# Output stage: loading the second token group's attention outputs earlier, and spacing its f16 forms

## The chip, the cores and the metric

The kernel runs on one core of a Trainium2 chip. The metric is the device time of one execution in microseconds (us). Five engines run side by side, each working through its own list of instructions in order: TensorE (PE in the profile; PEld are its weight loads), VectorE (DVE), ScalarE (ACT), GpSimd (POOL) and SyncE (SP), whose work here is to issue DMA transfers. An instruction that must wait for another engine holds up everything behind it in its own list. The kernel writes these lists itself, so the order of instructions on each engine is fixed when the program is built.

## The reference

One block of a bidirectional encoder: x is 2048 tokens of width 1024. A projection feeds two attention mixers, SiLU gates and merge gates. The change touches only the end:

```python
ya = ya.reshape(bsz, S, A_WIDTH) * jax.nn.silu(ga)      # attention outputs A
...
yb = yb.reshape(bsz, S, B_WIDTH) * jax.nn.silu(gb)      # attention outputs B
br_a = ya @ w_branch_a[layer]
br_b = yb @ w_branch_b[layer]
gates = jax.nn.sigmoid(mg.reshape(bsz, S, N_BRANCHES, D).astype(jnp.float32)
                       + b_merge[layer].astype(jnp.float32)).astype(x.dtype)
merged = gates[:, :, 0] * br_a + gates[:, :, 1] * br_b
x = x + merged @ w_out[layer]
```

## The kernel before

**Stages.** The first two thirds project the input and run the attention. Then the gates are computed from the projections (lines 1600 and 302, ended by the tanh of line 1526, and stored to DRAM as `mgd` from line 1530). The last stage, called the tail here, makes the two branch products, merges them, and makes the output product. The gated attention outputs lie transposed in DRAM as `ytd`, the weights of the branches in SBUF as the first parts of `bigh` and `bigl`, the output weights in DRAM as `wod`.

**Number format.** Every f32 matrix that enters a product is split into a high and a low f16 part, and a product is three f16 products. ScalarE makes the high part by scaling and rounding (`hi`, line 1757), VectorE the low part by subtracting the high part from the scaled value (`lo`, line 1761).

**Seven products for eight.** A block product of 2 x 2 blocks is made with seven products of sums of blocks. The right-hand blocks of a branch are two token halves by two channel halves, so a *token group* `s` (0 to 7) is the 128 tokens from 128 s and the 128 tokens from 1024 + 128 s. For each group and branch (s, k), `load` brings two tiles of 256 KB from `ytd` (line 1742), `sums` makes four sums of blocks on VectorE (line 1753, in two `tq` tiles), and seven pairs `hi`, `lo` make the seven forms. The forms `y0` of branch 0 and `y1` of branch 1 each have a ring of eight tiles. A form of group s + 1 therefore takes the tile of an earlier form, and waits until the product that read it is through. The two loaded tiles of branch k lie behind the weights in `WB[k]` and are overwritten by the next group's load, once all sums and forms of the group before are made.

**The order of products.** `Branch(s, k)` has seven products of 24 matmuls (line 1912), `Out(s)` seven products of 12 matmuls (line 1984). `run` interleaves them: products 5 and 6 of one part come between the first products of the next. The order is Branch(0, 0), Branch(0, 1), Branch(1, 0), Branch(1, 1), then for each s Out(s), Branch(s + 2, 0), Branch(s + 2, 1).

**What follows a product.** Some products end in a PSUM bank that a later one adds to. ScalarE copies a bank (`copy`, line 1834, into a `t` or `r` tile), VectorE adds a later state of a bank to it (`add`, line 1845), GpSimd multiplies with the gate tile `g` (line 1922), VectorE adds up the branches (`merge`, line 1929, and `last`, line 1933). `m_build` then makes the sums (line 1949) and forms (`mf`, lines 1953 and 1957) of the merged values for Out. Out's results are added to the tokens `xr` (`put`, line 1991) and stored (line 1994). A product whose bank is still to be copied or added waits.

**What sets the order.** Up to the gates' end a planner (`Plan`, `pl.add(name, engine, us, needs, rank, f)`) places steps: it starts a step when its needs are met and its engine is free, and picks by rank among those that could start. After that `at(t, f)` puts a step at a time written by hand, relative to `pos[0]`, where TensorE stands in the plan. Both only order the instructions in each engine's list: nothing waits for a time when the kernel runs. `y_steps(0, k)` plans group 0; `y_build(s, k, b, b0)` puts the load at `b0` (or at `b`), the sums from `b + Y_S` (4.0), and the forms 0.7 apart.

SP's list at the end of the gates is, in order: the load of (0, 1), three stores of gates, the four gate tiles of (0, 0) (line 1897, which can only start when the last gate product has read its weights, since they lie in the same memory), the loads of (1, 0) and (1, 1), the gate tiles of (0, 1), a last gate store, and then the seven 1 MB parts of the output weights (`wo_load`, line 1890) between gate tiles and tokens.

Of the kernel before, what the change touches and what calls it, by code (L numbers as in the profile page):

```python
# [30 lines left out]
S = 2048  # L31
# [14 lines left out]
def unit_order():  # L46
    us = [("A", 0, 0)]
    for p in range(4):
# [34 lines left out]
W_RAW, L_LAST = 14.0, 0.3  # L83
STD, W_EARLY, G_TH, G_SI, G_CP, K_AT = 5.2, 24.0, 2.0, 4.0, 1.0, (4, 17)
Y_S = 4.0
M_AT = {0: (1.0, (5.0, 6.6, 8.2, 9.8, 11.4, 13.0, 14.6)), 1: (1.0, (6.5, 8.7, 10.9, 13.1, 15.3, 17.5, 19.7)),
        7: (.7, (3.5, 5.4, 7.3, 9.2, 11.1, 13.5, 26.4))}
X_LD = ("g", 0, 1, 2, 3, "w0", 4, 5, "w1", 6, 7, 8, 9, 10, 11, 12, 13, "u")
# [18 lines left out]
def block_kernel(tc, x, w_units, w_gate, w_mrg, w_out, w_bra, w_brk, gain, qkg, sink, bias_a, bias_b, b_merge, out):  # L107
# [273 lines left out]
    def at(t, f, *args):  # L381
        seq[0] += 1
        heapq.heappush(heap, (t, seq[0], f, args))
# [3 lines left out]
    def until(t):  # L387
        while heap and heap[0][0] <= t:
            now[0], _, f, args = heapq.heappop(heap)
            f(*args)  # L390
# [121 lines left out]
    class Order:  # L512
# [17 lines left out]
        def run(self):  # L530
            while self.steps:
                best = {}
                for n, s in self.steps.items():
                    t = self.start(n)
                    if t is not None:
                        best.setdefault(s[0], []).append((t, s[3], n))
                eng, c = min(best.items(), key=lambda e: min(e[1])[0])
                t0 = min(c)[0]
                t, _, n = min((x for x in c if x[0] <= t0 + (0 if eng == "T" else X_US["look"])), key=lambda x: x[1])
                eng, us, _, _, f, args, _ = self.steps.pop(n)  # L540
                self.end[n] = self.free[eng] = t + us
                at(t, f, *args)
# [3 lines left out]
    n = 0  # L546
# [11 lines left out]
    for t in range(NT):  # L558
# [9 lines left out]
        for h in range(2):  # L568
            k = 2 * t + h
# [108 lines left out]
    class Pair:  # L678
# [85 lines left out]
        def hi(self):  # L764

            n = 2 * self.nh
            self.q = self.rw[:, :n * HD].rearrange("p (s h e) -> p s h e", s=2, e=HD)
            A.activation(self.sp[:, :, :self.nh, 0, :], self.q, AF.Copy)  # L768

        def lo(self):  # L770
            sp, nh = self.sp, self.nh
            V.tensor_tensor(sp[:, :, :nh, 1, :], self.q, sp[:, :, :nh, 0, :], OP.subtract)  # L772
# [456 lines left out]
    while t < NPAIR or heap or any(k >= t for k in fill):  # L1229
# [24 lines left out]
        pos = t  # L1254
# [38 lines left out]
    def tq():  # L1293
        return tp.tile([128, 512], F32, name="tq", bufs=2)
# [32 lines left out]
    class Plan:  # L1327
# [23 lines left out]
        def run(self):  # L1351
# [9 lines left out]
            for _ in range(len(self.steps)):  # L1361
# [20 lines left out]
    g_us = G_US  # L1382
    first = 0.0
    GR = 7 * MM
    pl = Plan({"fps": 8, "t2": 4, "tq": 2, "r2": 3, "t4": 3, "raw": 3, "w": 2, "yr": 4, "pc": 7},
              {"w": [[], [("p", 1, i) for i in range(7)]]})
# [347 lines left out]
    def y_parts(s, k):  # L1734

        r = {}

        def load():
            r[0] = y = [WB[k][h][:, 7168:].bitcast(F32).rearrange("p (c t) -> p c t", c=4) for h in range(2)]
            for h in range(2):  # L1740
                t0 = 128 * s + 1024 * h
                nc.sync.dma_start(out=y[h], in_=ytd[4 * k:4 * k + 4, :, t0:t0 + 128].rearrange("c p t -> p c t"))

        def sums(n):
            if n == 0:
                y = r[0]
                a11, a12, a21, a22 = y[0][:, 0:2], y[0][:, 2:4], y[1][:, 0:2], y[1][:, 2:4]
                u, v = (tq()[:].rearrange("p (s c n) -> p s c n", s=2, c=2) for _ in range(2))
                r[1] = (a11, u[:, 0], a12, u[:, 1], v[:, 1], v[:, 0], a22)
                r[2] = ((u[:, 0], a21, a22, OP.add), (u[:, 1], u[:, 0], a11, OP.subtract),  # L1750
                        (v[:, 1], a12, u[:, 1], OP.subtract), (v[:, 0], a11, a21, OP.subtract))
            o, a, b, op = r[2][n]
            V.tensor_tensor(o, a, b, op)

        def hi(i):
            yf[s, k, i] = f = yp.tile([128, 2, 2, 128], F16, name=f"y{k}")
            A.activation(f[:, 0], r[1][i], AF.Copy, scale=ysg[:])

        def lo(i):
            f = yf[s, k, i]  # L1760
            V.scalar_tensor_tensor(f[:, 1], r[1][i], ysg[:], f[:, 0], OP.mult, OP.subtract)

        return load, sums, hi, lo

    def y_build(s, k, b, b0=None):
        load, sums, hi, lo = y_parts(s, k)
        at(b if b0 is None else b0, load)
        for n in range(4):
            at(b + Y_S + .4 * n, sums, n)
        for n in range(7):  # L1770
            at(b + Y_S + .9 + .7 * n, hi, n)
            at(b + Y_S + 1.7 + .7 * n, lo, n)

    def y_steps(s, k):
        load, sums, hi, lo = y_parts(s, k)
        N = lambda *x: ("y", s, k) + x
        r = first + GR * LAST + 4 * STD + 2 * 7 * MM1 * s + 7 * MM1 * k
        pl.add(N("ld"), "S", 2 * g_us["dma"], [("wb", k, 0)] + [n + ("st",) for n in silus], r - 20, load, lag=4.5)
        for n in range(4):
            rel = [N("l", i) for i in range(7)]  # L1780
            pl.add(N("s", n), "V", g_us["a2"], [N("ld"), "yp"] + ([N("s", n - 1)] if n else []), r - 12 + .1 * n, lambda n=n: sums(n),
                   ring=[("tq", rel)] * 2 if n == 0 else ())
        for n in range(7):
            d = {1: 0, 3: 1, 4: 2, 5: 3}.get(n, 0)
            pl.add(N("h", n), "A", g_us["h2"], [N("s", d), "y2"] + ([N("h", n - 1)] if n else []), r - 9 + n, lambda n=n: hi(n))
            pl.add(N("l", n), "V", g_us["l2"], [N("h", n)], r - 8 + n, lambda n=n: lo(n))
# [8 lines left out]
           [("w", dc, "l", i) for dc in list(groups_of)[1:] for i in range(7)], 0, swap_y)  # L1795
    for k in range(2):
        y_steps(0, k)
    pl.run()
    while not end7:
        until(heap[0][0])  # L1800
    pos = [end7[0] + .01]
    y_build(1, 0, pos[0] + 6.0, pos[0] + .1)
    y_build(1, 1, pos[0] + 14.0, pos[0] + .2)
    until(pos[0])

    class Seven:
# [71 lines left out]
    def flush():  # L1878
        while pending:
            pos[0] += .3  # L1880
            late()
# [17 lines left out]
    class Branch(Seven):  # L1899
        n, mm_us = 7, MM1  # L1900
# [37 lines left out]
    def m_build(s, b):  # L1938
# [19 lines left out]

        d, e = M_AT[s if s in (0, 7) else 1]
        for n in range(4):  # L1960
# [5 lines left out]
    class Out(Seven):  # L1966
        n, mm_us = 7, MM
# [39 lines left out]
    def AB(s):  # L2007
        p = pos[0]
        at(p + (4.0 if s else 1.0), g_tiles, s, 1)
        if s == 0:  # L2010
            at(p + 9, g_tiles, 1, 0)
            for i in range(7):
                at(p + 2.0 + 5.5 * i, wo_load, i)
        run(Branch(s, 0))
        run(Branch(s, 1))

    AB(0)
    at(pos[0] + 9, outs[0].load, ((0, 0), (1, 1), (0, 1), (1, 0)))
    AB(1)
    for s in range(8):  # L2020
        p = pos[0]
        if s < 6:
            at(p + .1, g_tiles, s + 2, 0)
            y_build(s + 2, 0, p + 5.0)
            y_build(s + 2, 1, p + 14.0)
        if s < 7:
            at(p + (24.0 if s < 6 else 2.0), outs[s + 1].load, ((0, 0), (1, 1)))
            at(p + (31.0 if s < 6 else 15.5), outs[s + 1].load, ((0, 1),))
            at(p + (31.1 if s < 6 else 28.0), outs[s + 1].load, ((1, 0),))
        if s == 6:  # L2030
            flush()
        run(outs[s])
        if s < 6:
            AB(s + 2)
# [79 lines left out]
```

## Time and profile before

| | us |
|---|---|
| three runs: median (lowest to highest) | 1920.43 (1917.46 to 1922.58) |
| the profiled execution: its time | 1923.34 |
| the profiled execution: its span in the trace | 1920.9 |

The time of the profiled execution is 2.4 us above its span, which counts from its first to its last instruction. The tail fills the last 309 us of the span. Its first part by stretches of 10 us (busy time of each engine in each, and the share of the core's 16 DMA engines that was in use):

| stretch, us from the start | TensorE | VectorE | ScalarE | GpSimd | DMA share |
|---|---|---|---|---|---|
| 1600 to 1610 (gates) | 10.00 | 2.63 | 4.75 | 0.00 | 0.67 |
| 1610 to 1620 | 10.00 | 3.13 | 4.28 | 1.85 | 0.68 |
| 1620 to 1630 | 10.00 | 7.46 | 5.21 | 3.52 | 0.88 |
| 1630 to 1640 | 8.49 | 9.93 | 4.15 | 4.25 | 1.02 |
| 1640 to 1650 | 8.39 | 9.90 | 6.29 | 3.34 | 1.07 |
| 1650 to 1660 | 10.00 | 9.79 | 0.00 | 3.55 | 1.09 |
| 1660 to 1670 | 10.00 | 7.46 | 5.29 | 1.14 | 0.37 |
| 1670 to 1680 | 7.04 | 9.93 | 5.74 | 1.44 | 0.69 |

In a row of the timeline the columns are the start, the duration, the engine, the line, the operation, what it writes and reads, how many instructions are merged in the row, and in brackets the idle time of the engine before it with what ended it. Names in it are those of the tiles without their numbers.

### The profile page before, as it was taken

The numbers are of one execution on the slowest core, as the hardware profiler recorded it, in microseconds if no ns is written. First come the engines' busy times: TensorE is split into PE (matmuls) and PEld (weight loads), VectorE is DVE, ScalarE is ACT, GpSimd is POOL, SyncE is SP. The second block draws the span as 40 slices with busy tenths as digits, with TensorE's granted clock in tenths as the row PEclk, the third lists the DMA queues.
The fourth block names the chain that finished last, engine by engine and source line by source line (L and its number), as shares of the span: only waits on it lengthen the run. The fifth ranks groups of instructions, "written<-read, shape, count | busy, mean of one in ns | idle before, by whom it ended". The sixth has DMA issues, their size and how long they took to land.

```text
span 1920.9 us, 51094 instructions
## 1 busy us (share of the span) xinstructions
PE 1876.6 (98%) x19242; PEld 1439.4 (75%) x19242; DVE 1501.5 (78%) x3835; ACT 1251.2 (65%) x3015; POOL 579.1 (30%) x1363
## 2 busy tenths in 40 slices
PE   6999999999999999999999999999999999899998
PEld 4568987789999899988999898544444446676774
DVE  7679878986887889878789888657778644977885
ACT  8477768887777777777767766575675865433441
POOL 1034333443553435543455445200000001222121
PEclk9999999999999999999999999999999999999999
DMA  6259998988888679887888777776576557854551
GB/s 255 83 98 197 165 183 143 190 169 165 166 150 182 138 156 202 153 157 175 146 169 160 137 148 146 180 295 181 182 214 181 183 186 252 270 153 120 148 153 61
DMA packets 639351, 326.21 MB, mean 170 GB/s; under 512 B 459264, under 2 KB 589952, under 8 KB 636672
## 3 DMA queue, kind: packets, MB, share of 16 engines
q1 hardware_dynamic: 638960, 322.70, 72.6%
q8 instruction: 150, 2.46, 0.6%
q14 instruction: 97, 0.79, 0.2%
q10 hardware_dynamic: 144, 0.26, 0.0%
HBM read 139.08 MB, written 73.66 MB: 111 GB/s over the span
## 4 chain that ended last, share of the span: by engine, by line
PE 86%; DMA 6%; DVE 4%; ACT 2%; issue 1%; SPq 1%; POOL 0%; DVEq 0%; POOLq 0%
PE pj L695 42%; PE fps L1600 17%; PE fps L1984 7%; PE fps L1912 6%; PE s L845 5%; PE pv L894 4%; DMA pt<-p 2%; PE pj L350 2%; PE pj L302 1%; PE fps L302 1%; DMA kq<-spl 1%; DMA bigl<-ytd 1%; PE pt L958 1%; DMA bigl<-sd 1%; PE s L480 0%
## 5 line engine op out<-in xcount | busy, mean ns | idle before, releaser
L695 PE MATMUL pj<-wl,XH 128*128 128x128 f16 (+2 forms) x2816 | 715.9, 268 | 0.0
L695 PE MATMUL pj<-wh,XL 128*128 128x128 f16 (+2 forms) x2816 | 712.2, 269 | 0.0
L695 PE MATMUL pj<-wh,XH 128*128 128x128 f16 (+2 forms) x2816 | 709.4, 268 | 0.0
L695 PEld LDWEIGHTS <-XH 128*128 128x128 f16 x5632 | 575.4, 112 | 54.6
L695 PEld LDWEIGHTS <-XL 128*128 128x128 f16 x2816 | 316.0, 112 | 24.0
L860 DVE CUSTOM_DVE_ANT_0 pr<-s,b,ubuf 128x256 f32<-128x256 f32 (+3 forms) x512 | 218.9, 465 | 42.1 <-PE s L845 39.5
L877 DVE SCALAR_TENSOR_TENSOR p<-pr,p 128x512 f16<-128x512 f32 (+2 forms) x256 | 195.8, 765 | 51.5 <-ACT p L873 48.6
L762 POOL TENSOR_TENSOR rw<-rw,g 128x128 f32<-128x128 f32 (+1 forms) x224 | 149.2, 686 | 202.5 <-DVE rw L755 170.2
L1922 POOL TENSOR_TENSOR g<-g,t 128x512 f32<-128x512 f32 x32 | 48.5, 1515 | 529.5 <-DVE t L1845 529.5
L1600 PEld LDWEIGHTS <-wh 128*128 128x128 f16 x1064 | 104.2, 99 | 123.5 <-issue 0.6
L713 ACT ACTIVATE rw<-pj 128x256 f32<-128x256 f32 (+1 forms) x224 | 87.4, 390 | 130.0 <-PE pj L695 129.3
L777 POOL COPY spl<-spl 128x256 f16<-128x256 f16 (+1 forms) x224 | 96.7, 461 | 244.5 <-DVE spl L772 244.5
L873 ACT ACTIVATE p<-pr 128x512 f16<-128x512 f32 (+2 forms) x256 | 157.7, 616 | 14.6 <-DMA pt<-p 10.3
L1912 PE MATMUL fps<-y,bigh 128*128 128x128 f16 x1792 | 153.8, 219 | 3.9 <-DVE r L1845 3.9
L1984 PE MATMUL fps<-WO,mf 128*128 128x512 f16 x672 | 151.9, 382 | 3.8 <-DVE xr L1991 3.8
L1912 PE MATMUL fps<-y,bigl 128*128 128x128 f16 x896 | 151.8, 219 | 0.0
L845 PE MATMUL s<-kq 128*128 128x128 f16 (+1 forms) x1856 | 148.2, 218 | 3.6 <-DMA kq<-spl 2.7
L1912 PEld LDWEIGHTS <-bigh 128*128 128x128 f16 x1792 | 139.1, 98 | 11.6 <-issue 4.3
L845 PEld LDWEIGHTS <-kq 128*128 128x128 f16 x2016 | 130.9, 98 | 19.9 <-issue 4.5
L894 PE MATMUL pv<-vt,pt 128*128 128x65 f16 (+1 forms) x2784 | 131.9, 193 | 8.1 <-DMA pt<-p 7.4
L894 PEld LDWEIGHTS <-pt 128*128 128x128 f16 x3024 | 119.3, 98 | 24.1 <-DMA pt<-p 12.1
L768 ACT ACTIVATE spl<-rw 128x512 f16<-128x512 f32 (+1 forms) x112 | 72.0, 643 | 80.3 <-POOL vt L724 70.2
(252 smaller groups left out, 3816.7 us busy)
## 6 DMA issues: line engine op xcount, KB each, us to landing
wraw<-in_w_units_dram SPq DMA_DIRECT2D x56, 384.0 KB, 4.8
g<-mgd SPq DMA_DIRECT2D x64, 256.0 KB, 4.9
wraw<-in_w_mrg_dram SPq DMA_DIRECT2D x45, 256.0 KB, 4.2
mgd<-t SPq DMA_DIRECT2D x43, 256.0 KB, 2.9
zd<-z SPq DMA_DIRECT2D x128, 66.0 KB, 2.0
zz<-zd SPq DMA_DIRECT2D x64, 132.0 KB, 3.4
xt<-in_x_dram SPq DMA_DIRECT2D x16, 512.0 KB, 8.2
ytd<-yo SPq DMA_DIRECT2D x32, 256.0 KB, 3.3
```

What stands on the lines that cost most here:

```text
L695: out.append(lambda lhs=lhs, rhs=rhs, ch=ch, a=a, b=b, k=k: T.matmul(ps[:, a:b], lhsT=lhs[:, ch, :], rhs=rhs[:, ch, a:b], start=(k == 0), ...
L713: A.activation(self.rw[:, n * i:n * i + n], self.ps[i][:, :n], AF.Copy)
L762: G.tensor_tensor(q[:, i, :un.nq, :], q[:, i, :un.nq, :], g, OP.mult)
L777: G.tensor_copy(sp[:, i, nh:, :, :], sp[:, i, nq:nh, ::-1, :])
L845: T.matmul(self.sv[j][:, o:o + k1 - k0], lhsT=q[:, h, :], rhs=kt[:, un.nq + kh + v * un.nk, k0:k1], start=(v == 0), stop=(v == 1))
L860: V.tensor_tensor_reduce(out=self.pv[:, j, self.p0:self.p0 + W], in0=self.sv[j], in1=un.bias[:, self.h0 + j, self.b0:self.b0 + W], scale=I ...
L873: A.activation(self.sp[:, :128 * n], self.pr, AF.Copy, scale=PSC)
L877: V.scalar_tensor_tensor(self.sp[:, 128 * n:], self.pr, PSC, self.sp[:, :128 * n], OP.mult, OP.subtract)
L894: T.matmul(self.po[:, j, :w], lhsT=p[:, n * j + s, :], rhs=un.v[key][:, vh, c0:c0 + w], start=(k == 0 and s == 0), stop=(k == 2 and s == n ...
L1600: T.matmul(b[k][:], lhsT=w[:, i, ch, :], rhs=xform(PROD[i][0], lo, ch, q), start=(i < 3 and n == 0), stop=(n == 11), skip_group_check=True)
L1912: out.append(lambda p=p, c=c, wl=wl, yl=yl, n=n: T.matmul(ps[:, 128 * p:128 * p + 128], lhsT=w[wl][:, i, c, p, :], rhs=y[:, yl, c, :], sta ...
L1984: out.append(lambda p=p, ml=ml, wl=wl, k=k: T.matmul(ps[:], lhsT=m[:, ml, p, :], rhs=WO[:, i, wl, p, :], start=(fresh and k == 0), stop=(k ...
```

## The change

The loads of (1, 0) and (1, 1) become planner steps on SP that need only the seven low forms of (0, k), with a rank that puts them behind all other work that could be issued. The sums and forms of group 1 are no longer placed by `y_build`. For (1, 0) the sums stand from 0.2 after the gates' end and the forms from 0.9, 1.6 apart; for (1, 1) from 13.0 and 14.0, 1.6 apart. In the loop over s, the load of (s + 2, 0) moves from 5.0 to 0.05 after the start of Out(s), which is ahead of the gate tiles at 0.1. The constants of `wo_load` get a name and keep their values.

```diff
+Y_1 = (.2, .9, 1.6), (13.0, 14.0, 1.6)
+WO_AT = 2.0, 5.5
...
     for k in range(2):
         y_steps(0, k)
+    ahead = [y_parts(1, k) for k in range(2)]
+    for k in range(2):
+        pl.add(("y", 1, k, "ld"), "S", 2 * g_us["dma"], [("y", 0, k, "l", i) for i in range(7)], 1e4 + k, ahead[k][0], lag=4.5)
     pl.run()
...
     pos = [end7[0] + .01]
-    y_build(1, 0, pos[0] + 6.0, pos[0] + .1)
-    y_build(1, 1, pos[0] + 14.0, pos[0] + .2)
+    for (load, sums, hi, lo), (a, b, d) in zip(ahead, Y_1):
+        for n in range(4):
+            at(pos[0] + a + .2 * n, sums, n)
+        for n in range(7):
+            at(pos[0] + b + d * n, hi, n)
+            at(pos[0] + b + d * n + .8, lo, n)
...
-                at(p + 2.0 + 5.5 * i, wo_load, i)
+                at(p + WO_AT[0] + WO_AT[1] * i, wo_load, i)
...
-            y_build(s + 2, 0, p + 5.0)
+            y_build(s + 2, 0, p + 5.0, p + .05)
             y_build(s + 2, 1, p + 14.0)
```

SP's list at the gates' end, from the second of the three gate stores on (`ytd` into `bigh`, `bigl` is a load of attention outputs, `mgd` from `t` a gate store, `g` from `mgd` gate tiles), before:

```order
L1530 DMA mgd<-t_27977 128x512
L1530 DMA mgd<-t_28007 128x512
L1897 DMA g<-mgd 128x4x128 x4
L1742 DMA bigh<-ytd 128x4x128
L1742 DMA bigl<-ytd 128x4x128
```

and now, with line numbers that the diff has moved:

```order
L1532 DMA mgd<-t_27977 128x512
L1744 DMA bigh<-ytd 128x4x128
L1744 DMA bigl<-ytd 128x4x128
L1532 DMA mgd<-t_28009 128x512
L1906 DMA g<-mgd 128x4x128 x4
```

The load of (1, 0) has moved past one gate store and four gate tiles; the load of (1, 1) follows the gate tiles as before.

VectorE's list after the last form of (0, 1) (`y0` are forms of branch 0, the lines 1845 and 1854 the `add`), before:

```order
L1845 TENSOR_TENSOR t2_28092<-fps_28122,t2_28092 128x512
L1845 TENSOR_TENSOR t2_28174<-fps_28093,t2_28174 128x512
L1753 TENSOR_TENSOR tq_28277<-bigl_27732 128x256
L1753 TENSOR_TENSOR tq_28277<-tq_28277,bigh_27731 128x256
L1753 TENSOR_TENSOR tq_28278<-bigh_27731,tq_28277 128x256
L1845 TENSOR_TENSOR r2_28121<-fps_28053,r2_28121 128x512
L1753 TENSOR_TENSOR tq_28278<-bigh_27731,bigl_27732 128x256
L1761 SCALAR_TENSOR_TENSOR y0_28300<-bigh_27731,ubuf_70,y0_28300 128x256
L1845 TENSOR_TENSOR t2_28228<-fps_28293,t2_28228 128x512
```

and now:

```order
L1755 TENSOR_TENSOR tq_28061<-bigl_27732 128x256
L1755 TENSOR_TENSOR tq_28061<-tq_28061,bigh_27731 128x256
L1755 TENSOR_TENSOR tq_28062<-bigh_27731,tq_28061 128x256
L1755 TENSOR_TENSOR tq_28062<-bigh_27731,bigl_27732 128x256
L1763 SCALAR_TENSOR_TENSOR y0_28083<-bigh_27731,ubuf_70,y0_28083 128x256
L1763 SCALAR_TENSOR_TENSOR y0_28127<-tq_28061,ubuf_70,y0_28127 128x256
L1854 TENSOR_TENSOR t2_28100<-fps_28133,t2_28100 128x512
```

and, behind four more forms and `add`s, up to the first sum of (1, 1):

```order
L1763 SCALAR_TENSOR_TENSOR y0_28269<-tq_28062,ubuf_70,y0_28269 128x256
L1854 TENSOR_TENSOR r2_28132<-fps_28055,r2_28132 128x512
L1763 SCALAR_TENSOR_TENSOR y0_28310<-bigl_27732,ubuf_70,y0_28310 128x256
L1854 TENSOR_TENSOR t2_28248<-fps_28315,t2_28248 128x512
L1755 TENSOR_TENSOR tq_28362<-bigl_27874 128x256
```

The four sums and seven forms of (1, 0) now stand between the forms of (0, 1) and the fourth `add`; the sums of (1, 1) follow it at once. Before, six low forms of (1, 0) and three other instructions came between that `add` and the sums of (1, 1). ScalarE's list changes in the same way: it now reads (lines 1759 are `hi`, 1843 are `copy`)

```order
L1759 ACTIVATE y0_28083<-bigh_27731,ubuf_70 128x256
L1843 ACTIVATE t2_28100<-fps_28055 128x512
L1759 ACTIVATE y0_28127<-tq_28061,ubuf_70 128x256
L1843 ACTIVATE r2_28132<-fps_28101 128x512
L1759 ACTIVATE y0_28162<-bigh_27731,ubuf_70 128x256
L1843 ACTIVATE t2_28189<-fps_28055 128x512
```

where five copies stood together ahead of the first high form of (1, 0). SP's list at the start of Out(0), before and now:

```order
L1890 DMA WO<-wod 128x4096
L1897 DMA g<-mgd 128x4x128 x4
L1890 DMA WO<-wod 128x4096
L1742 DMA bigh<-ytd 128x4x128
L1742 DMA bigl<-ytd 128x4x128
```

```order
L1899 DMA WO<-wod 128x4096
L1744 DMA bigh<-ytd 128x4x128
L1744 DMA bigl<-ytd 128x4x128
L1906 DMA g<-mgd 128x4x128 x4
L1899 DMA WO<-wod 128x4096
```

The load of (2, 0) has moved past four gate tiles and one part of the output weights. In the later groups it has moved past the four gate tiles in the same way.

## The prediction

> **What bounds the kernel now.** I began with the busy shares of the page.
>
> ```profile
> PE 1876.6 (98%) x19242; PEld 1439.4 (75%) x19242; DVE 1501.5 (78%) x3835; ACT 1251.2 (65%) x3015; POOL 579.1 (30%) x1363
> ```
>
> TensorE works 98% of the span, so a change of order can win only what it loses. For the part that the diff touches, the view of waits from 1611 to 1681 us has two rows for TensorE, and its timeline shows where they lie:
>
> ```profile
> PE fps L1912 <- DVE r L1845: 3.1, 2, 1.6
> PE fps L1984 <- DVE xr L1991: 3.0, 1, 3.0
> ```
>
> ```profile
> 1611.69 0.28 PE L1912 MATMUL fps<-y,bigh 128*128 128x128 f16 x2
> ...
> 1636.15 0.27 PE L1912 MATMUL fps<-y,bigh 128*128 128x128 f16 x2 [1.51 <-DVE r L1845]
> ...
> 1647.30 0.27 PE L1912 MATMUL fps<-y,bigh 128*128 128x128 f16 x2 [1.61 <-DVE r L1845]
> ...
> 1676.79 4.39 PE L1984 MATMUL fps<-WO,mf 128*128 128x512 f16 x12 [2.96 <-DVE xr L1991]
> 1681.01 0.27 PE L1912 MATMUL fps<-y,bigh 128*128 128x128 f16 x2
> ```
>
> Three gaps: 1.51, 1.61 and 2.96 us. The twelve matmuls behind the third take 1681.01 - 1676.79 = 4.22 us. The chain of waits shows their normal pace, and the windows the reason:
>
> ```profile
> 1681.17 10.72 PE fps L1912 x192
> 1691.89 5.18 PE fps L1984 x24
> ```
>
> ```profile
> 1611.69:1622.40 10.71, 10.71 (x193) 10.71 (x192) 1.44 (x3) 4.77 (x8) 2.54 (x2) 1.00 0.76 217
> 1622.40:1677.00 54.60, 48.52 (x653) 39.47 (x650) 51.47 (x84) 23.55 (x47) 15.11 (x10) 1.00 0.87 281
> 1676.79:1680.20 3.41, 3.41 (x9) 1.18 (x9) 3.41 (x6) 1.82 (x3) 1.44 (x1) 0.51 0.75 228
> ...
> 1677.00:1877.00 200.00, 200.00 (x2319) 147.85 (x2318) 160.33 (x279) 74.90 (x144) 49.35 (x34) 0.99 0.49 143
> ```
>
> (Columns: length; busy time of PE, PEld, DVE, ACT, POOL; granted clock; DMA share; GB/s.) 24 matmuls of Out take 5.18 us, so twelve take 2.59; behind the gap the clock was 0.51, which cost 4.22 - 2.59 = 1.63 us. In all 1.51 + 1.61 + 2.96 + 1.63 = 7.71 us are lost here, and that is the most this change can win. A product of 24 matmuls takes 10.72 / 8 = 1.34 us.
>
> VectorE ends all three gaps. The windows say why: it was busy 1.44 of the first 10.71 us and 51.47 of the next 54.60. Its rows:
>
> ```profile
> 1615.97 0.69 DVE L1845 TENSOR_TENSOR t<-fps,t 128x512 f32<-128x512 f32 x1 [4.22 <-ACT r L1834]
> 1618.65 0.69 DVE L1845 TENSOR_TENSOR t<-fps,t 128x512 f32<-128x512 f32 x1 [1.99 <-PE fps L1912]
> 1622.47 0.43 DVE L1753 TENSOR_TENSOR tq<-bigl 128x256 f32<-128x256 f32 x1 [3.13 <-DMA bigl<-ytd]
> ...
> 1629.28 0.68 DVE L1933 TENSOR_TENSOR g<-fps,g 128x512 f32<-128x512 f32 x1
> ...
> 1630.28 0.68 DVE L1929 TENSOR_TENSOR g<-g 128x512 f32<-128x512 f32 x1
> ...
> 1631.27 0.68 DVE L1845 TENSOR_TENSOR t<-fps,t 128x512 f32<-128x512 f32 x1
> ...
> 1632.32 1.38 DVE L1753 TENSOR_TENSOR tq<-tq,bigh 128x256 f32<-128x256 f32 x1
> ...
> 1646.56 0.68 DVE L1845 TENSOR_TENSOR r<-fps,r 128x512 f32<-128x512 f32 x1
> ...
> 1662.51 0.43 DVE L1753 TENSOR_TENSOR tq<-bigl 128x256 f32<-128x256 f32 x1 [2.72 <-DMA bigl<-ytd]
> 1662.85 0.75 DVE L1991 SCALAR_TENSOR_TENSOR xr<-fps,ubuf,xr 128x512 f32<-128x512 f32 x1
> ...
> 1675.99 0.75 DVE L1991 SCALAR_TENSOR_TENSOR xr<-fps,ubuf,xr 128x512 f32<-128x512 f32 x1
> ```
>
> It idles 4.22 + 1.99 + 3.13 = 9.34 us while the load of (1, 0) is under way. Then it hardly pauses (51.47 + 2.72 = 54.19 of 54.60), but for the 2.72 us that it waits for the load of (2, 0), from 1659.8 to 1662.5, and it has the `xr` that TensorE needs at 1676.74.
>
> **Part 1: the load of (1, 0).**
>
> ```profile
> 1602.34 0.72 ACT L1529 ACTIVATE t<-t,ones 128x512 f32<-128x512 f32 x1
> ...
> 1607.52 0.72 ACT L1529 ACTIVATE t<-t,ones 128x512 f32<-128x512 f32 x1
> ...
> 1613.33 0.58 ACT L1834 ACTIVATE t<-fps 128x512 f32<-128x512 f32 x1
> ```
>
> ```profile
> bigl<-ytd SPq DMA_DIRECT2D x1, 256.0 KB, 7.4
> ```
>
> ```profile
> 1614.55 7.47 DMA bigl<-ytd
> ```
>
> (ScalarE's timeline; the DMA issues from 1599.2 to 1611, with the median time to landing at the row's end; the chain of waits.) Each gate store waits for ScalarE's L1529. The load now follows the second store (freed at 1603.06) instead of the third (1608.24) and four gate tiles, so it is issued from about 1603.4. The load of (0, 1), the one in that view, took 7.4 us; I take 7.5, so the two halves of (1, 0) land by about 1611.5 instead of 1614.55 + 7.47 = 1622.0. Its two issues take 0.5 us each on SP, which was waiting for ScalarE until 1608.24: nothing. It also takes 512 KB out of the full DMA stretch; at 281 GB/s the transfers behind land up to 1.9 us sooner. The load of (1, 1) still follows the gate tiles, but nothing else: issued near 1614.5 it lands by 1622, and is wanted at 1624.4 (part 2).
>
> **Part 2: the forms of (1, 0).** The VectorE work between 1622.47 and 1631.27 is the four sums and seven low forms of (1, 0), two `add`s, and L1933 and L1929, which are 0.60 each from start to start and stay. So 8.80 - 1.20 = 7.60 us leave the full stretch. Free of collisions the eleven instructions need about 5 us (0.43 or 0.48 each), beside the 9.34 us of idle time: nothing, if the load is there. If that cover were gone they would cost those 5 us again.
>
> The sums of (1, 1) now follow the `add` of the ninth product: 1611.69 + 9 x 1.34 + 0.69 = 1624.4. What came from 1631.27 to 1676.74 is 45.47 us; less the 2.72 of waiting (part 3), plus the 1.20 that stay, 43.95. VectorE without a pause would have the deciding `xr` at 1668.4. It will pause once, since TensorE is only 3.12 us earlier without gaps one and two:
>
> ```profile
> 1656.49 5.34 PE L1984 MATMUL fps<-WO,mf 128*128 128x512 f16 x24
> ```
>
> The first twelve of these end at 1659.08, and the `xr` of 1662.85 needs them: at 1659.08 - 3.12 = 1656.0. From there 1676.74 - 1662.85 = 13.9 us lead to 1669.9. TensorE reaches the third gap at 1676.79 - 2.96 - 3.12 = 1670.7. All three gaps close, the last with 0.8 us to spare.
>
> Gap two: the `add` of 1646.56 came 15.29 us after 1631.27; from 1624.4, with 1.20 more, it comes at 1640.9, and TensorE needs it at 1647.30 - 1.61 - 1.51 = 1644.2. Gap one has a shorter list ahead and the same lead.
>
> **Collisions.**
>
> ```profile
> 1632.03 1.39 POOL L1922 TENSOR_TENSOR g<-g,t 128x512 f32<-128x512 f32 x1 [3.75 <-DVE t L1845]
> ```
>
> VectorE's sum of 1632.32, started inside this GpSimd multiplication, took 1.38 us instead of 0.43, until the multiplication's end. Such a hold costs 0.95. How many fall into the new order no row shows: the bounds are all ten multiplications of the window of 54.60 us free (9.5 us gained) and two more holds than before (1.9 lost). I take the same number, since the same instructions meet. The Trainium skill (SBUF — State Buffer, section Who interferes with whom) speaks against the change here: a VectorE instruction with two inputs in SBUF and a GpSimd instruction that reads SBUF shut each other out for the whole instruction, whichever starts first. The rows agree. By the rule alone, forms moved beside the first multiplications are held there too, and if two holds lie behind 1624 as extras the sum is 1.1 us worse.
>
> **Part 3: the load of (2, 0).**
>
> ```profile
> 1645.76 0.49 SPq L1890 DMA_DIRECT2D WO<-wod  x1
> 1647.87 4.98 SPq L1897 DMA_DIRECT2D g<-mgd  x4
> 1652.90 2.11 SPq L1890 DMA_DIRECT2D WO<-wod  x1
> 1655.06 0.43 SPq L1742 DMA_DIRECT2D bigh<-ytd  x1
> ```
>
> ```profile
> WO<-wod SPq DMA_DIRECT2D x7, 1024.0 KB, 8.6
> ...
> bigl<-ytd SPq DMA_DIRECT2D x3, 256.0 KB, 7.0
> ```
>
> ```profile
> 1678.20 1.44 POOL L1922 TENSOR_TENSOR g<-g,t 128x512 f32<-128x512 f32 x1 [17.07 <-DVE t L1845]
> ```
>
> (SP's timeline; the DMA issues from 1612 to 1662; GpSimd's timeline.) It stood behind gate tiles that wait for tiles still in use. Ahead of them it goes out at about 1646.3 and lands by 1653.8; VectorE asks for it at 1659.8 less its lead of 1646.56 - 1640.9 = 5.7 us, at 1654.1: the 2.72 us go. The gate tiles come about 1 us later, and GpSimd was idle 17.07 us before it used them; the last weights, issued 1 us later than 1652.90, land near 1662.5 and are read in the product at 1670.7. In the later groups, where the same swap is made, TensorE worked 200.00 of 200.00 us to 1877: nothing.
>
> **Part 4: the ring.** ScalarE's high forms 1 to 6 of (1, 0) wait for the products 1 to 5 of the branch and the eighth, which ends at 1611.69 + 8 x 1.34 = 1622.4. Behind that last wait stands the copy of the tenth product, ready at 1625.1: nothing. The first high form stands ahead of the copy that ran at 1613.33: it delays it by 0.5 us, to an end at 1614.4, and the fourth product, which adds to that bank, starts at 1611.69 + 3 x 1.34 = 1615.7.
>
> **The sum.** 7.7 us, less 0.7 for the last gap, whose 0.8 us to spare is less than one hold: 7.0. From the profiled execution, 1923.34 - 7.0 = 1916.3 us; it lies 2.9 above the median, so the median becomes 1913.4, or 0.36% less.
>
> **The rivals.**
>
> *VectorE stays late.* For it: 51.47 of 54.60 us busy, so any pause or hold pushes the rest. Only the 2.72 us of the load go, `xr` comes at 1674.0, TensorE has arrived at 1670.7 and still loses 3.3 + 1.63: gain 3.12 + 2.96 - 3.3 = 2.8, that is 1917.6. Against it: 7.60 us of work leave.
>
> *The change does not do what it says: the work does not move.* The low forms of (1, 0) stand among the `add`s of the first products and wait for high forms, and these for the ring. If VectorE comes out of this as late as before, at 1631.3, only the order of the list has changed: 1920. Against it: the last tile is free at 1622.4, two microseconds before VectorE can take up the sums of (1, 1).
>
> *Slower: ScalarE is held at the first form.* If the load landed where it did, at 1622.0, the first high form would hold the copy behind it, to an end at 1622.0 + 0.5 + 0.58 = 1623.1, and the fourth product would wait from 1615.7: 7.4 us, and 1.6 of half clock. Gaps one and two (3.1) would be hidden by it, the third not: 5.9 slower, 1926. It decides from a landing after 1614.6, 11.2 us after issue; the loads above took 7.
>
> **How the numbers follow.** Forecast 0.66, VectorE late 0.22, nothing 0.07, slower 0.05. Below 0.3%, here 5.8 us, a measurement of this kernel cannot be told from no change. The forecast's own range is 1912.0 to 1916.0 and lies mostly under 1914.7; with the part of the second case close to it, faster has 0.60, same 0.35, slower 0.05. The range of 1910.8 to 1918.6 takes in the second case and the holds.
>
> **What would show it.** Right: no wait of TensorE on `r` L1845 between 1620 and 1660; the load of (1, 0) issued near 1603; VectorE busy from 1612; no row of 2.72 before the sums of (2, 0); granted clock 1.00 from 1670 to 1682. Wrong: a gap of TensorE at the fourth product, or one over 2 us at the last product of Out(0).

## The result, and the profile after

| | before | changed |
|---|---|---|
| median of 12 runs each, side by side | 1920.49 us (1915.94 to 1923.32) | 1914.97 us (1912.31 to 1916.61) |
| profiled execution | 1923.34 us, span 1920.9 | 1916.55 us, span 1914.3 |
| tail: from the first product of the first branch to the end of the span | 309.2 us (from 1611.69) | 300.9 us (from 1613.39) |

The changed kernel takes 0.9974 of the time of the one before (95% interval 0.9966 to 0.9982), 5.5 us less. 1913.4 was predicted, with its own range of 1912.0 to 1916.0: the direction and the three places were right, the gain of 7.0 us was too large. The profile shows a puzzle at once: between the two profiled executions the tail became 8.3 us shorter, more than the medians gained. What varies there is the subject of the experiments.

The windows of the changed kernel (length; busy time of PE, PEld, DVE, ACT, POOL; granted clock; DMA share; GB/s), over the first eight products, then to 1671.5, then past the place of the old third gap:

```profile
1613.39:1624.10 10.71, 10.71 (x193) 10.71 (x192) 5.41 (x12) 6.64 (x13) 2.83 (x2) 1.00 0.89 253
1624.10:1671.50 47.40, 47.40 (x647) 38.90 (x644) 45.92 (x74) 20.25 (x40) 15.27 (x10) 1.00 0.93 305
1671.50:1682.00 10.50, 10.50 (x158) 9.09 (x156) 9.47 (x16) 4.84 (x8) 3.76 (x3) 1.00 0.61 195
```

TensorE is busy in all of each stretch, at full clock: the three gaps and the half clock are gone. VectorE, busy 1.44 us of the first 10.71 before, is now busy 5.41. Its timeline shows the moved work and the two places that decided:

```profile
1613.18 0.42 DVE L1755 TENSOR_TENSOR tq<-bigl 128x256 f32<-128x256 f32 x1
...
1625.65 0.69 DVE L1854 TENSOR_TENSOR t<-fps,t 128x512 f32<-128x512 f32 x1 [0.25 <-PE fps L1921]
1626.26 0.55 DVE L1755 TENSOR_TENSOR tq<-bigl 128x256 f32<-128x256 f32 x1
1626.84 1.38 DVE L1755 TENSOR_TENSOR tq<-tq,bigh 128x256 f32<-128x256 f32 x1
...
1656.37 0.41 DVE L1755 TENSOR_TENSOR tq<-bigl 128x256 f32<-128x256 f32 x1
1657.54 0.75 DVE L2000 SCALAR_TENSOR_TENSOR xr<-fps,ubuf,xr 128x512 f32<-128x512 f32 x1 [0.76 <-PE fps L1993]
...
1670.68 0.74 DVE L2000 SCALAR_TENSOR_TENSOR xr<-fps,ubuf,xr 128x512 f32<-128x512 f32 x1
```

(Lines behind the edit have moved: L1753 is now L1755, L1845 is L1854, L1991 is L2000, L1912 is L1921, L1984 is L1993.) The sums of (1, 0) start at 1613.18 and those of (2, 0) at 1656.37, both without a wait for a load. On SP's timeline the loads stand where the diff puts them:

```profile
1605.22 0.38 SPq L1744 DMA_DIRECT2D bigh<-ytd  x1
1605.69 0.64 SPq L1744 DMA_DIRECT2D bigl<-ytd  x1
...
1644.52 0.38 SPq L1744 DMA_DIRECT2D bigh<-ytd  x1
1645.33 0.37 SPq L1744 DMA_DIRECT2D bigl<-ytd  x1
1647.86 5.97 SPq L1906 DMA_DIRECT2D g<-mgd  x4
```

What TensorE still loses in the tail are two short waits at the very end, which the kernel before has as well:

```profile
1871.85 0.27 PE L1921 MATMUL fps<-y,bigh 128*128 128x128 f16 x2 [0.78 <-DVE r L1854]
1907.87 2.32 PE L1993 MATMUL fps<-WO,mf 128*128 128x512 f16 x10 [0.84 <-DVE xr L2000]
```

### The profile page after: what moved, and what is told of

Its sections match the earlier page's. It is cut to its first block, busy times and chain, and to the rows that moved or that the text cites. A ratio compares the mean times of both kernels' runs of the same rounds, so it can differ in the third digit from the quotient of the medians.

```text
span 1914.3 us, 51103 instructions
## 1 busy us (share of the span) xinstructions
PE 1873.9 (98%) x19242; PEld 1438.9 (75%) x19242; DVE 1500.7 (78%) x3835; ACT 1250.4 (65%) x3015; POOL 579.0 (30%) x1363
## 3 DMA queue, kind: packets, MB, share of 16 engines
q8 instruction: 150, 2.46, 0.6%
## 4 chain that ended last, share of the span: by engine, by line
PE 90%; DMA 5%; DVE 2%; ACT 1%; issue 1%; POOL 0%; SPq 0%; DVEq 0%; POOLq 0%
PE pj L697 43%; PE fps L1602 17%; PE fps L1921 8%; PE fps L1993 8%; PE s L847 5%; PE pv L896 4%; DMA pt<-p 2%; PE pj L352 2%; PE pj L304 1%; PE fps L304 1%; DMA kq<-spl 1%; PE pt L960 1%; DMA bigl<-sd 1%; DVE pr L862 0%; PE s L482 0%
## 5 line engine op out<-in xcount | busy, mean ns | idle before, releaser
L1921 PE MATMUL fps<-y,bigh 128*128 128x128 f16 x1792 | 153.5, 219 | 0.8 <-DVE r L1854 0.8
L1921 PE MATMUL fps<-y,bigl 128*128 128x128 f16 x896 | 151.7, 219 | 0.0
L1993 PE MATMUL fps<-WO,mf 128*128 128x512 f16 x672 | 150.3, 379 | 0.8 <-DVE xr L2000 0.8
L1921 PEld LDWEIGHTS <-bigh 128*128 128x128 f16 x1792 | 139.0, 98 | 8.2 <-issue 0.9
```

The source lines that it names most:

```text
L1921: out.append(lambda p=p, c=c, wl=wl, yl=yl, n=n: T.matmul(ps[:, 128 * p:128 * p + 128], lhsT=w[wl][:, i, c, p, :], rhs=y[:, yl, c, :], sta ...
L1993: out.append(lambda p=p, ml=ml, wl=wl, k=k: T.matmul(ps[:], lhsT=m[:, ml, p, :], rhs=WO[:, i, wl, p, :], start=(fresh and k == 0), stop=(k ...
```

## The experiments

The runs of one set stood beside runs of the kernel before on the same chip: its median was 1918.69 us (35 runs) for the first four kernels, 1917.85 (20) for the next four and 1918.48 (17) for the last three. Because the start of the tail moves from one execution to the next, the length of the tail is compared too: it starts when TensorE begins the first product of the first branch, and ends with the span.

### The kernel before, profiled again, five profiles in all

No edit, four more executions of the same program:

> The kernel before, unchanged, profiled a second time, to see how far its tail is the same from one execution to the next. Tail here means from the first product of the first branch to the end; in the first profile it starts at 1611.69 and holds three gaps of TensorE (1.51, 1.61, 2.96) and 1.63 of half clock, 7.71 in all; in the changed kernel's profile it starts at 1613.39 and holds none of them. Theory A (the gaps are the same in every execution, and what varies is the part before the tail): again 7.7 +- 0.5 in the tail, and the start of the tail moves with the time of the execution. Theory B (the profiled execution of before was a bad one of its kind; the third gap and the half clock come and go, which is why the median gained 5.5 and not 7.7): an execution nearer to the median has a third gap under 2.4 us, no half clock, and 3.5 to 6 us lost in all. The timed ratio is 1.000 within 0.001 in either case.

> The kernel before, profiled a third time. Theory B: the load of (1, 0) decides. If it lands 8.1 to 8.7 us after the tail's first matmul (as in the second profile) the three gaps lose 3 to 4 us and there is no half clock; if it lands after 9.5 us, 5 us or more. Rival (the gaps vary for another reason): a late landing with small gaps, or the reverse.

> The kernel before, profiled a fourth time, for the spread of what its tail loses. Theory B: the pair of landing of the load of (1, 0) and loss lies on the line of the others: 3.6 to 4 lost for a landing up to 9.1 us after the first product, 7.7 for 10.3 us, between them for landings between.

> The kernel before, profiled a fifth time; expected as in the fourth.

The second, third, fourth and fifth profile were of executions of 1915.08, 1919.37, 1918.52 and 1916.76 us; 12 timed runs of the first of them had a median of 1918.97 and a ratio of 1.0001 (0.9991 to 1.0011). TensorE's timeline of the second profile has all three gaps, two of them smaller:

```profile
1631.14 0.27 PE L1912 MATMUL fps<-y,bigh 128*128 128x128 f16 x2 [0.41 <-DVE r L1845]
...
1642.29 0.27 PE L1912 MATMUL fps<-y,bigh 128*128 128x128 f16 x2 [1.60 <-DVE r L1845]
...
1670.27 0.59 PE L1984 MATMUL fps<-WO,mf 128*128 128x512 f16 x2 [1.56 <-DVE xr L1991]
```

and VectorE's timeline of the same execution says why; the two rows are its waits for the loads of (1, 0) and of (2, 0), 3.13 and 2.72 in the first profile:

```profile
1616.93 0.43 DVE L1753 TENSOR_TENSOR tq<-bigl 128x256 f32<-128x256 f32 x1 [1.49 <-DMA bigl<-ytd]
...
1655.72 0.69 DVE L1753 TENSOR_TENSOR tq<-bigl 128x256 f32<-128x256 f32 x1 [0.94 <-DMA bigl<-ytd]
```

All five, with the same rows read out of each (us):

| profile of before | tail starts | tail | wait for (1, 0) | gap one | gap two | wait for (2, 0) | gap three |
|---|---|---|---|---|---|---|---|
| first | 1611.69 | 309.2 | 3.13 | 1.51 | 1.61 | 2.72 | 2.96, half clock |
| second | 1607.79 | 304.9 | 1.49 | 0.41 | 1.60 | 0.94 | 1.56 |
| third | 1611.87 | 305.1 | 1.89 | 0.40 | 1.59 | 1.45 | 1.78 |
| fourth | 1611.07 | 305.2 | 1.62 | 0.41 | 1.60 | 1.50 | 1.83 |
| fifth | 1607.72 | 306.6 | 2.78 | 1.16 | 1.59 | 2.11 | 2.46 |

The part ahead of the tail moves by 4.2 us, and it moves as much in the changed kernel (1613.39 and, below, 1609.20). But the tail moves too, by 4.3 us, so theory A of the first text falls. Gap one follows the wait for (1, 0): it is that wait less 1.62, and at least 0.40. Gap three follows the wait for (2, 0): it is 0.24 to 0.62 longer than that wait. Gap two is always 1.6. The first profile, on which the prediction rests, had the longest waits of the five and alone had the half clock. The mean of the five tails is 306.2 us.

Theory B of the later texts, that a later load of (1, 0) goes with a larger loss, fits these five: the first sum of (1, 0) starts 9.1, 9.3, 9.5, 10.4 and 10.8 us after the first product, and the gaps with the half clock come to 3.6, 3.8, 3.8, 5.2 and 7.7 us. That the load of (1, 0) alone decides is not shown by that, since the wait for (2, 0) grows along with it; the swapped loads below are the test.

### One part of the change alone

The load of (2, 0) alone:

```
-            y_build(s + 2, 0, p + 5.0)
+            y_build(s + 2, 0, p + 5.0, p + .05)
```

> The kernel before with one line of the change: the load of (2, 0), and of (s + 2, 0) in the later groups, goes ahead of the gate tiles on SP's queue; the loads and forms of group 1 stay as they were. Theory A (the prediction's terms add up: VectorE's wait of 2.72 us for this load is one term of its own): gaps one and two stay at 1.5 and 1.6, the third shrinks by 2.72 to 0.2-0.5 and the half clock behind it goes; 4.3 us less than before in the profile, about 1916 to 1917 in the median. Rival (VectorE is late mainly from the work of group 1, and what it does not wait here it waits elsewhere): third gap over 2 us, at most 1 us gained, 1919.5 to 1920.5.

Measured: 1916.85 us, ratio 0.9991 (0.9981 to 1.0002), tail 304.9 us. VectorE does not wait for that load any more, and TensorE's timeline has:

```profile
1635.59 0.27 PE L1912 MATMUL fps<-y,bigh 128*128 128x128 f16 x2 [1.24 <-DVE r L1845]
...
1646.74 0.27 PE L1912 MATMUL fps<-y,bigh 128*128 128x128 f16 x2 [1.61 <-DVE r L1845]
...
1673.84 0.59 PE L1984 MATMUL fps<-WO,mf 128*128 128x512 f16 x2 [0.68 <-DMA g<-mgd]
```

The third gap fell to 0.68 and the first two stayed, as theory A of this run said. But the medians differ by 1.8 us, which is not clear of noise (the interval takes in 1), and not by 4.3: the usual wait that is removed is 1.5 us and not 2.72, and the half clock is not usually there. That 1916.85 falls into the 1916 to 1917 of its text is luck: the kernel before had 1918.69 here and not 1920.5. (The third row names a gate tile's transfer as the releaser. VectorE's `xr` of that place ended at 1673.79, 0.05 ahead of the matmul, so it is taken to be the last of the things waited for.)

The changed kernel without that one line, that is, the early loads and forms of group 1 alone:

```
-            y_build(s + 2, 0, p + 5.0, p + .05)
+            y_build(s + 2, 0, p + 5.0)
```

> The changed kernel without that one line: the load of (2, 0) goes back behind the gate tiles; loads and forms of group 1 stay early. Theory A: gaps one and two stay closed (3.1 us gained); VectorE asks for the load some 5.7 us earlier than in the kernel before and the load lands where it did or a little sooner, so it waits there 5 to 7 us instead of 2.72, the third gap is 2 to 4 us and has a stretch of half clock behind it: 4 to 5.5 us more than the changed kernel, 1918.5 to 1920.5 in the median. Rival (the early forms alone give VectorE enough lead to swallow the wait): no third gap, time within 1 us of the changed kernel's 1915.

Measured: 1916.06 us, ratio 0.9990 (0.9979 to 1.0001), tail 303.6 us. Gaps one and two are gone. VectorE waits longer for the load of (2, 0), and one gap is left, in this order in the timelines of VectorE and TensorE, with the window behind it:

```profile
1656.60 0.43 DVE L1755 TENSOR_TENSOR tq<-bigl 128x256 f32<-128x256 f32 x1 [3.88 <-DMA bigl<-ytd]
```

```profile
1670.88 0.59 PE L1993 MATMUL fps<-WO,mf 128*128 128x512 f16 x2 [2.64 <-DVE xr L2000]
```

```profile
1670.88:1674.29 3.41, 3.41 (x27) 1.99 (x27) 3.41 (x6) 1.82 (x3) 1.44 (x1) 1.00 0.67 227
```

The rival (the lead of the early forms swallows the wait) falls: what VectorE gains ahead of the load it waits for at the load, 3.88 us instead of 0.94 to 2.72. Theory A was too high in size: the wait is not 5 to 7 us, and the gap of 2.64 us left the clock at 1.00.

The changed kernel with the forms of group 1 put back, that is, all three loads early and nothing else:

```
-    for (load, sums, hi, lo), (a, b, d) in zip(ahead, Y_1):
+    for (load, sums, hi, lo), b in zip(ahead, (6.0, 14.0)):
...
-            at(pos[0] + a + .2 * n, sums, n)
+            at(pos[0] + b + Y_S + .4 * n, sums, n)
...
-            at(pos[0] + b + d * n, hi, n)
-            at(pos[0] + b + d * n + .8, lo, n)
+            at(pos[0] + b + Y_S + .9 + .7 * n, hi, n)
+            at(pos[0] + b + Y_S + 1.7 + .7 * n, lo, n)
```

> The changed kernel with the forms of group 1 put back to their old times, that is, only the three loads are early. Theory A (the prediction's part 2: work has to leave VectorE's full stretch): VectorE no longer waits for the load of (1, 0), but its forms still run behind the adds in the full stretch; at gaps one and two together 1 to 4 us remain, the tail is 302 to 305 us, 2 to 3 us slower than the changed kernel. Rival (only the loads count): no gaps, a tail of 301, the time of the changed kernel within 1 us.

Measured: 1916.99 us, ratio 0.9995 (0.9986 to 1.0005), tail 304.0 us. VectorE waits for no load of groups 1 and 2, and yet TensorE's timeline has:

```profile
1632.43 0.27 PE L1921 MATMUL fps<-y,bigh 128*128 128x128 f16 x2 [0.40 <-DVE r L1854]
...
1643.58 0.27 PE L1921 MATMUL fps<-y,bigh 128*128 128x128 f16 x2 [1.61 <-DVE r L1854]
...
1670.66 0.59 PE L1993 MATMUL fps<-WO,mf 128*128 128x512 f16 x2 [0.67 <-DVE xr L2000]
```

The first two are the smallest values of the table above, and the third is that of the run with the load of (2, 0) alone (0.68). So 0.4, 1.6 and 0.7 come from the order of VectorE's list, in which the forms of (1, 0) stand in the full stretch, and only what goes beyond them comes from late loads. Moving the forms takes the rest: 304.0 becomes 300.9. By the tails the early loads are worth 306.2 - 304.0 = 2.2 us of the 5.3 and the moved forms 3.1. The medians of this run and of the changed kernel beside it lie further apart (1916.99 and, below, 1912.43); they hold the part ahead of the tail too, and why they differ by more is not shown.

### The loads of group 1 in the other order

```
-    y_build(1, 0, pos[0] + 6.0, pos[0] + .1)
+    y_build(1, 0, pos[0] + 6.0, pos[0] + .3)
```

> The kernel before with the loads of (1, 0) and (1, 1) in the other order on SP's queue, nothing else: the load that VectorE wants first lands where the second landed, 1.6 us later. Theory B (before's loss hangs on when this load lands: 3.6 to 3.8 in tail gaps for a landing 8.7 to 9.1 us after the first product, 7.7 for 10.3 us): landing at 10.3 to 12, gap one 1.5 to 3, gap three near 3 or more with half clock behind it, 7.5 to 9.5 lost in the tail in every execution; the median 2 to 4 us over that of before. Rival (the landing is not what decides): time and gaps as before, within 1 us.

Measured: 1917.64 us, ratio 0.9993 (0.9983 to 1.0004), tail 306.4 us: not slower, against what theory B said. VectorE's waits for the two loads, and TensorE's gaps:

```profile
1623.75 0.42 DVE L1753 TENSOR_TENSOR tq<-bigl 128x256 f32<-128x256 f32 x1 [3.28 <-DMA bigl<-ytd]
...
1662.44 0.42 DVE L1753 TENSOR_TENSOR tq<-bigl 128x256 f32<-128x256 f32 x1 [1.38 <-DMA bigl<-ytd]
```

```profile
1637.42 0.27 PE L1912 MATMUL fps<-y,bigh 128*128 128x128 f16 x2 [1.66 <-DVE r L1845]
...
1648.57 0.27 PE L1912 MATMUL fps<-y,bigh 128*128 128x128 f16 x2 [1.60 <-DVE r L1845]
...
1676.71 1.46 PE L1984 MATMUL fps<-WO,mf 128*128 128x512 f16 x6 [1.72 <-DVE xr L1991]
```

Gap one is as long as a late load makes it (3.28 - 1.62 = 1.66). But VectorE then asks for the load of (2, 0) later too (48.2 us after the first product, where the profiles with the small gap one have 47.0), waits only 1.38 us for it, and gap three is short: 5.0 us are lost in the three gaps, not 7.5 to 9.5. So the late load of (1, 0) does not decide the whole loss, as theory B had it: up to the landing of (2, 0), a delay in gap one is given back at gap three. The two waits have to be read one by one. Why the same transfers land sooner in one execution than in another was not tried, and stays open.

### The slower rival, made to happen

The changed kernel, with the planner's two steps for the loads taken out and the loads put back at the start of the tail; the forms stay early:

```
-    for k in range(2):
-        pl.add(("y", 1, k, "ld"), "S", 2 * g_us["dma"], ...
...
+        at(pos[0] + (.1 if a < 1 else .15), load)
```

> The changed kernel with the two loads of group 1 issued where the kernel before issued them, at the start of the tail, while the forms stay early in the lists of ScalarE and VectorE: the prediction's slower rival, made to happen. Its working: the load lands at 1622, the first high form holds the copy behind it on ScalarE, the fourth product waits 7.4 us and 1.6 of half clock follow, the later gaps are hidden by it: about 9 us more than the changed kernel, 1922 to 1926, slower than before. Rival (ScalarE or the copy has more room than the rival's working says, so early loads matter little): a gap under 2 us at the fourth product and a time within 3 us of the changed kernel's 1915.

Measured: 1921.08 us, ratio 1.0010 (1.0000 to 1.0020), tail 307.4 us, 6.5 more than the changed kernel. ScalarE's and TensorE's timelines, and the windows of the gap and of the 3.41 us behind it:

```profile
1621.15 0.51 ACT L1759 ACTIVATE y<-bigh,ubuf 128x256 f16<-128x256 f32 x1 [6.37 <-DMA bigh<-ytd]
1621.56 0.58 ACT L1842 ACTIVATE t<-fps 128x512 f32<-128x512 f32 x1
```

```profile
1622.19 0.37 PE L1920 MATMUL fps<-y,bigh 128*128 128x128 f16 x2 [4.96 <-ACT t L1842]
```

```profile
1617.20:1622.19 4.99, 0.03 (x1) 0.00 (x0) 0.32 (x1) 0.99 (x2) 0.00 (x0) 0.94 0.99 290
1622.19:1625.60 3.41, 3.41 (x38) 3.41 (x38) 3.08 (x8) 2.04 (x5) 0.52 (x1) 0.59 1.06 294
```

The mechanism is the one of the prediction's rival: the first high form waits for the load, the copy stands behind it, and the fourth product behind the copy. No other gap is left before the two of the tail's end. The gap is 4.96 us and not 7.4, since ScalarE could form 8.1 us after the tail's start (1621.15 - 1613.04), where the prediction had 10.3. Most of that is the load itself: issued 2.3 us after the tail's start in both profiles, its first half took 5.8 us to land here and 7.4 in the prediction's profile. The rest is that the form needs the first half alone, and the prediction had it wait for both. The run is 2.4 us slower than the kernel before by the medians (the interval starts at 1.0000), and its median lies under the 1922 to 1926 that its text expected. The early load is what the early forms need.

### The changed kernel again, and the two gaps that are left

> The changed kernel, unchanged, profiled a second time and timed beside the kernel before on the chip of the experiments. Theory B of the first experiment (what the change removes is the 3.6 to 7.7 us that the tail of before loses, as the load of (1, 0) takes 5.8 to 7.5 us): whatever that load takes in this execution, the tail has none of the three gaps and is again 300.9 +- 0.4 us from the first product to the end of the span; the median is 5 to 6 us under that of before. Rival (the changed kernel's tail varies in the same way and the first profile was a lucky one): a gap of over 0.5 us at one of the three places.

No edit. Measured: 1912.43 us, ratio 0.9971 (0.9961 to 0.9981) to the kernel before, 5.4 us less by the medians. The profiled execution took 1911.97 us, 4.6 less than the first one of this kernel, but its tail starts at 1609.20, 4.2 earlier, and is 300.9 us long again:

```profile
1609.20:1671.20 62.00, 62.00 (x871) 52.08 (x870) 55.21 (x92) 29.29 (x57) 19.56 (x13) 1.00 0.89 290
```

The changed tail does not vary, in two profiles. Nor does the load's new place cost anything that shows ahead of the tail: in the five profiles with the early load of (1, 0) the tail starts at 1610.7 in the mean, in the eight without it at 1610.9, each with a spread of 4 to 5 us.

The second run gives the last product of branch (7, 1) and of the last Out a bank of its own, for the two gaps that are left at the tail's end (`...` stands for lines that are left out):

```
...
-            if i < 3:
+            if i < 3 or i == 6 and self.fresh:
                 self.b[k] = bank()
-            return self.matmuls(i, self.b[k], i < 3)
+            return self.matmuls(i, self.b[k], i < 3 or i == 6 and self.fresh)
...
+            if i == 5 and self.fresh:
+                self.put(1, 0, b[0])
...
+            self.fresh = (s, k) == (7, 1)
...
+            if i == 5 and self.fresh:
+                b, g, self.u = self.b[0], self.g(1, 0), t2()
+                at(now[0] + .3, lambda: V.tensor_tensor(self.u[:], b[:], g, OP.mult))
...
+            if self.fresh:
+                at(now[0] + .21, lambda: V.tensor_tensor(g, g, self.u[:], OP.add))
...
+    outs[7].fresh = True
```

> The changed kernel, and in it the last product of the last branch (7, 1) and of the last Out goes to a bank of its own instead of adding to the bank that VectorE still reads; VectorE adds the two with one more instruction each, which runs beside the product. The profile of the changed kernel shows two losses left in the tail there, 0.78 and 1.00 us. Theory: both go, the tail is 1.8 us shorter, 299.1 us, and the median 1.5 to 2 us under that of the changed kernel. Rival (the extra instruction behind the last product, or the later start of the sums of merge 7, gives it back): a tail over 300.3.

Measured: 1910.46 us (5 runs), ratio 0.9963 (0.9951 to 0.9975) to the kernel before. The profile shows no wait of TensorE in the tail, which is 298.9 us long, 2.0 less than the changed kernel's: both losses went, as the theory said. Against the changed kernel's 8 runs the median is 2.0 lower too, but so few runs do not settle it; what speaks for it is the tail of one profile, 2.0 us under one that came out the same twice.

## Why the prediction was right in kind and too large in size

**What bounds the kernel: right, from one unlucky execution.** The gaps, their places and their releaser were right, and VectorE's lateness made them, for they go when its work and its waits do. What failed is the step from "7.71 us in the profiled execution" to the median. The five profiles have a mean tail of 306.2 us, the first one 309.2. The prediction took the 2.9 us by which that execution lay above the median for noise outside the gaps; the tail alone was 3.0 above its mean. The mean tail less the changed tail is 306.2 - 300.9 = 5.3, and the medians gained 5.5 and 5.4. Of the term that was too large, the 7.71 us, gaps one and three and the half clock were the parts that a usual execution does not have in full: in three of the five profiles they are 0.40 or 0.41 us, 1.56 to 1.83 us, and nothing.

The prediction gave its largest chance, 0.60, to a gain of more than 5.8 us; the gain of 5.5 fell just short of it. Its statement that a difference below 0.3% cannot be told from none did not hold either: the interval around 0.26% runs from 0.18 to 0.34%.

**A gap costs a little more than its row says.** The difference of the first two profiles, 8.3 us, is more than "the most this change can win", 7.71. The wait in a row runs from the end of the matmul before. Two neighbouring rows of the changed kernel's TensorE:

```profile
1870.86 0.22 PE L1921 MATMUL fps<-y,bigl 128*128 128x128 f16 x1
1871.85 0.22 PE L1921 MATMUL fps<-y,bigh 128*128 128x128 f16 x1 [0.78 <-DVE r L1854]
```

The first lasts 0.22 us, but without a wait the second would start 10.72 / 192 = 0.056 us after it and not 0.22. So the gap of 0.78 costs 1871.85 - 1870.86 - 0.056 = 0.93, and each gap behind such a matmul about 0.16 more than its row says; with three, 7.71 becomes 8.2. The same sum fits the other runs. Take 300.9, add the gaps of the run, 0.16 for each, and the half clock where there is one (1.63 in the first profile, and 3.41 x (1 - 0.59) = 1.4 in the run of the slower rival). This gives the tails of all five profiles of before and of the five runs with a part of the change or with moved loads, each within about 0.1 us, so little else in the tail is lost or won.

**Part 1, the load of (1, 0): right, with room.** Issued 8.2 us ahead of the tail's first product (1613.39 - 1605.22; predicted 8.3), and no longer waited for. The DMA issues from 1603 to 1612 give 4.8 us to landing, where the prediction took 7.5:

```profile
bigl<-ytd SPq DMA_DIRECT2D x1, 256.0 KB, 4.8
```

The sums ran at 1613.18, as soon as VectorE was through with the forms of (0, 1).

**Part 2, the forms: right.** Predicted were the sums of (1, 1) 12.7 us after the start of the tail, one pause, and the deciding `xr` done 58.2 us after it. The profile has the sums at 1626.26, 12.9 after; the pause of 0.76 at 1657.54; and the `xr` done at 1670.68 + 0.74, 58.0 after. TensorE began the product behind it at 1671.81 without a wait, 58.4 after the start of the tail and not 59.0 as predicted (1670.7), since gaps one and two had cost more than their rows. So only 0.4 us were to spare and not 0.8; no hold came, and the 0.7 us taken off for the last gap were not needed. That they brought the forecast nearer to the median was luck. That the forms themselves must move, and not only the loads, is shown by the run with the forms put back (304.0 against 300.9).

**Collisions: roughly the same.** The row of 1626.84 is one: 1.38 instead of 0.43, again a sum that started inside a multiplication on GpSimd. It ended 0.27 us behind it (the prediction's sum 0.28 behind, and not at its end):

```profile
1626.49 1.46 POOL L1931 TENSOR_TENSOR g<-g,t 128x512 f32<-128x512 f32 x1
```

VectorE had the deciding `xr` done within 0.2 us of the predicted time, so no extra holds are seen behind 1624.

**Part 3, the load of (2, 0): mechanism right, size wrong.** The wait put at 2.72 us is 0.94 to 2.72 in five profiles, and the 1.63 of half clock came in one of them. VectorE asked for the load at 1656.37 and did not wait. The two parts do not simply add: the early forms alone make the wait for this load longer (3.88), and the early load alone leaves the gaps of the list.

**Part 4, the ring: right.** Nothing of it reached TensorE. ScalarE's last form, number 6 counted from 0, did wait, without cost:

```profile
1624.31 0.51 ACT L1759 ACTIVATE y<-bigl,ubuf 128x256 f16<-128x256 f32 x1 [0.74 <-PE fps L1921]
```

**The rivals.** "VectorE stays late" did not come true in the whole change, and came true when either half was left out. "The work does not move" is refuted by 5.41 us of VectorE work in the first eight products. The slower rival is real once the loads are late, but smaller: 2.4 us above the kernel before by the medians, where the prediction had 5.9, and 6.5 above the changed kernel by the tails, where 7.4 and 1.6 make 9.0. With the loads early it has no place.

## What to carry to other kernels

Before a gap's size goes into a sum, profile the same kernel two or three times: where a load ends the wait, the gap is as long as that load happened to take, and an execution that lies above the median may lie there because of the gaps themselves. When a list of work and a load both hold the same consumer, find the floor that each leaves alone; removing one lets the consumer wait longer at the other. And measure by the stage: here the time from the stage's start to the end repeated to 0.1 us in two profiles of the changed kernel, while whole runs moved by 4.

## What was not expected of the hardware

The clock halved behind TensorE gaps of 2.96 and 4.96 us (0.51 and 0.59 in the 3.41 us that follow) and not behind gaps of 2.64 and 2.46 us (1.00 behind either; the second is gap three of the fifth profile of before, its window is shown below). The Trainium skill (TensorE: Matmul & The Clock Gate, section HAM oscillation — how this bites in real kernels) gives the rule as no idle gaps of TensorE over about 3.4 us; here 2.96 was already too long (3.12 with the 0.16 of the section above), and the measurement decides. Each of these gaps was seen in one execution, so where between 2.64 and 2.96 the limit lies, and whether it is always the same, is not shown.

```profile
1671.82:1675.23 3.41, 3.40 (x27) 1.98 (x27) 3.41 (x6) 1.84 (x3) 1.44 (x1) 1.00 0.72 232
```

The load of (1, 0), behind the same transfers on the same queue, kept VectorE waiting between 1.49 and 3.13 us in five executions of the same program, and that of (2, 0) between 0.94 and 2.72. Gap three followed its wait nearly one for one, and gap one did so where its wait was above 2 us, in a tail that is otherwise fixed. What made the transfers land later in one execution than in another stays open.
